# Unit-length removal keys of an RWKV-7 recurrence, moved from the recurrence units to the key and value stages

## The chip, the core and the metric

The kernel runs on one core of a Trainium2 chip. A core has five engines that run side by side, each working through its own instructions in order: TensorE (PE; PEld is its loading of weights), VectorE (DVE), ScalarE (ACT), GpSimd (POOL) and SyncE (SP), which here issues nearly all DMAs. They wait for each other through semaphores. The metric is the device time of one execution in microseconds; all times are from the profile, the runs or the trace.

## The reference

The model has two layers over 256 frames of 2048 channels (32 heads of 64), float32 throughout: an RWKV-7 time mixing layer and a forgetting-attention layer, each followed by a SwiGLU channel mixer. The change touches the time mixing, whose core is

```python
rkv = jnp.einsum('pbtc,pcd->pbtd', xm[:3], w_rkv)
r, k, v = rkv[0], rkv[1], rkv[2]
w_log = -jax.nn.softplus(-(w0 + jnp.tanh(xw @ w1) @ w2).astype(f32)) - 0.5
decay = jnp.exp(-jnp.exp(w_log))
a = jax.nn.sigmoid(a0 + (xa @ a1) @ a2)
g = jax.nn.sigmoid(xg @ g1) @ g2
kk = (k * k_k).reshape(B, T, H, N).astype(f32)
kk = kk / jnp.maximum(jnp.sqrt(jnp.sum(kk * kk, axis=-1, keepdims=True)), 1e-12)
k = k * (1.0 + (a - 1.0) * k_a)
...
y = wkv7_scan(rh, wh, kh, vh, -kk, kk * ah)
```

with the state update `S_t = S_{t-1} diag(w_t) + (S_{t-1} a_t) b_t^T + v_t k_t^T`, `y_t = S_t r_t`. The vector `kk` is the removal key: the direction in which the state forgets, scaled to unit length in each head.

## The kernel before

Every large product is a GEMM over weights that are streamed from DRAM. `Stream` (lines 58 to 185) holds a list of all GEMMs in order. SP loads pieces of 512 KB into three stage buffers `st`; each piece has two blocks of 128 x 512. ACT rounds a block to its high half `wh` (L149) and DVE makes the low half `wl` (L150), up to six blocks ahead of PE. For each block and each of two tiles of 128 frames PE does three matmuls (L182 to L184): high by high, high by low, low by high. After each such triple `tick` gives every active generator one step: this is how other work is woven into a GEMM. A `yield` ends a step. At most four generators are active in the key and value stages, eight later; others wait in a queue.

The program is then laid out by a scheduler, which takes the instructions with their dependencies and writes an order for each engine, so an instruction can stand some way from where its step was. The buffers of a pool are reused in turn; the wait for the last reader of a buffer is added by the framework.

The time mixing has these stages:

1. `begin` (L383) normalises the input, transposes it and makes the operands of the k GEMMs.
2. The GEMMs k0 to k3. `keep_k` copies their results to `K`. From k1 on `early` (L510) is woven in: the token-shift mix of the values (`xm`, L374 to L381), then three low-rank products (`lora`, L442), whose operands `xlh` and `xll` DVE and ACT make just ahead of the matmuls L464 to L466.
3. The GEMMs v0 to v3. The mix for r is woven in; the values go to DRAM (`vdram`, L545), and `centred` (L495) sends them once more, less their head means (`wdram`, L507).
4. The GEMMs r0 to r3 with the small decay and gate GEMMs, then the output projection. Into these four pipelines are woven over eight units, a unit being one column group `g` of 512 channels (eight heads) and one tile `t`: `prepare` (L580) makes the decays and the scaled operands of a unit, `solve` and `merge` invert its triangular systems, `chain` carries the state, `post` normalises the outputs. They pass on to each other through the set `done`.

In `prepare` a unit's removal keys take six operations: `kk` = k times `vk` (L594, DVE), its square (L596, ACT), the sum over a head (L610, DVE), a lower bound (L611, DVE), the power of -1/2 (L612, POOL) and the scaling (L633, DVE). L634 and L638 then use `kk`. `vk` is the group's row of the parameter `a_k_k`, broadcast over the partitions, loaded with `va` and `vr` when r is finished (L953). The buffer `kk` is there once, so a unit's `kk` can only be written when the unit before has read its own for the last time (L646).

The pools that matter: `pre` holds two buffers each of `f2` and `u2` (used by `begin`, `f2` also by `centred`), `lw` two of each small tile.

Of the kernel before, what the change touches and what calls it, by code (L numbers as in the profile page):

```python
# [8 lines left out]
F32 = mybir.dt.float32  # L9
F32R = mybir.dt.float32r  # L10
BF16 = mybir.dt.bfloat16
AF = mybir.ActivationFunctionType
ALU = mybir.AluOpType
AX = mybir.AxisListType
# [3 lines left out]
P = 128  # L18
T = 256
D = 2048  # L20
KT = D // P
H = 32
N = 64
# [184 lines left out]
def hybrid_kernel(ctx, tc, const, x, a_norm_g, a_mix, a_w_rkv, a_w0, a_w1, a_w2, a_a0, a_a1, a_a2,  # L208
# [127 lines left out]
    with ExitStack() as actx:  # L336
        a1 = actx.enter_context(tc.tile_pool(name="a1", bufs=1))
        rv = actx.enter_context(tc.tile_pool(name="rv", bufs=2))
        vdram = dram.tile([T, D], F32, name="vdram")
        wdram = dram.tile([T, D], F32, name="wdram")  # L340
        loraw = {}

        with ExitStack() as bctx:
# [151 lines left out]
            def centred(vt, at):  # L495
# [11 lines left out]
                nc.sync.dma_start(wdram[at], wt)  # L507

            def early():
                fetch()  # L510
                fetch()
                yield from differences()
                yield from mixed(2, xv, "xv")
                yield from lora(LORA, 3, lambda ps: halves("w", LORA, ps[0:LORA, 0:T], AF.Tanh))
                yield from lora(LORA, 4, lambda ps: halves("a", LORA, ps[0:LORA, 0:T]))
                yield from lora(GLORA, 5, gate_halves)
                done.add(("lora", 0))
# [19 lines left out]
            xr = pair("xa")  # L537
            S.add(mixed(0, xr, "xr"))
            for g in range(4):
                ps = S.gemm(f"v{g}", lhs_of(xv), ready=lambda kt: has("xv", kt))  # L540
                for t in range(2):
                    vt = rv.tile([P, 512], F32, name="rv")
                    nc.scalar.copy(vt[:, :], ps[t][:, :])
                    at = slice(t * P, (t + 1) * P), slice(g * 512, (g + 1) * 512)
                    nc.sync.dma_start(vdram[at], vt[:, :])  # L545
                    S.add(centred(vt, at))
            S.until(lambda: not S.act and not S.pend)

        with ExitStack() as bctx:
# [31 lines left out]
            def prepare():  # L581
                for i, (g, t) in enumerate(order):
                    yield from wait(("r", g))
                    tw, ta = wat[g][0][t], wat[g][1][t]
                    vk, va, vr = vec[g][:3]
                    k = K[g][:, t, :]
# [6 lines left out]
                    kk = u1.tile([P, 512], F32, name="kk")  # L593
                    nc.vector.tensor_tensor(kk[:, :], k, vk[:, :], op=ALU.mult)  # L594
                    sq = u1.tile([P, 512], F32, name="rr")
                    nc.scalar.activation(sq[:, :], kk[:, :], AF.Square)  # L596
                    yield
# [10 lines left out]
                    S.give(2)  # L608
                    n8 = u1.tile([P, 8], F32, name="n8")
                    nc.vector.tensor_reduce(n8[:, :], h4(sq[:, :]), AX.X, ALU.add)  # L610
                    nc.vector.tensor_scalar(n8[:, :], n8[:, :], 1e-24, None, op0=ALU.max)  # L611
                    nc.gpsimd.tensor_tensor(n8[:, :], n8[:, :], pw[:, :], op=ALU.pow)  # L612
                    yield
# [18 lines left out]
                    yield  # L632
                    nc.vector.tensor_tensor(h4(kk[:, :]), h4(kk[:, :]), n8[:, :].unsqueeze(2).broadcast_to([P, 8, N]), op=ALU.mult)  # L633
                    nc.vector.scalar_tensor_tensor(Wp, kk[:, :], -1.0, Wp, op0=ALU.mult, op1=ALU.mult)  # L634
# [236 lines left out]
            def post(i, g, t, Y, bon):  # L871
# [3 lines left out]
                yield from wait(("g2", g))  # L875
                vg, vb = vec[g][3:]
                b8 = lambda a: a.unsqueeze(2).broadcast_to([P, 8, N])
# [66 lines left out]
            for g in range(4):  # L944
# [4 lines left out]
                for t in range(2):  # L949
                    a = rv.tile([P, 512], F32, name="rv")  # L950
                    nc.scalar.copy(a[:, :], ps[t][:, :])
                    rts[g].append(a)
                vec[g] = [bc(v, g, nm) for v, nm in ((a_k_k[0], "vk"), (a_k_a[0], "va"), (a_r_k[0].rearrange("h n -> (h n)"), "vr"))]  # L953
                nc.scalar.mul(vec[g][1][:, :], vec[g][1][:, :], 0.5)
                ps = S.gemm(f"w2{g}", lambda kt: tuple(loraw["w"]))
# [451 lines left out]
```

## Time and profile before

| what | us |
|---|---|
| median of 3 runs | 2602.72 (2599.71 to 2609.24) |
| the profiled execution, its own time | 2608.68 |
| span of the profiled execution, first to last instruction | 2606.8 |
| PE busy | 2558.9 |
| DVE busy | 1693.5 |
| ACT busy | 1412.3 |
| POOL busy | 90.3 |
| the eight scalings L633 start at | 245.2 to 516.5 |

"Busy" is the time in which an engine had an instruction in work. Matmuls overlap, so PE can look busy while it is not at its pace; its pace is read from the number of matmuls in a stretch. A group's row gives its count, the shortest, median and longest duration in ns, and when the first and the last of it start. The chain of waits is followed back from the last instruction: at each step to what released it, or to the instruction before it on its engine. An engine's row of a wait names who ended it, its sum, how often, and the longest.

### The profile page before, as it was taken

The numbers are of one execution on the slowest core, as the hardware profiler recorded it, in microseconds if no ns is written. First come the engines' busy times: TensorE is split into PE (matmuls) and PEld (weight loads), VectorE is DVE, ScalarE is ACT, GpSimd is POOL, SyncE is SP. The second block draws the span as 40 slices with busy tenths as digits, with TensorE's granted clock in tenths as the row PEclk, the third lists the DMA queues.
The fourth block names the chain that finished last, engine by engine and source line by source line (L and its number), as shares of the span: only waits on it lengthen the run. The fifth ranks groups of instructions, "written<-read, shape, count | busy, mean of one in ns | idle before, by whom it ended". The sixth has DMA issues, their size and how long they took to land.

```text
span 2606.8 us, 40879 instructions
## 1 busy us (share of the span) xinstructions
PE 2558.9 (98%) x15160; PEld 2091.2 (80%) x15160; DVE 1693.5 (65%) x3041; ACT 1412.3 (54%) x2613; POOL 90.3 (3%) x73
## 2 busy tenths in 40 slices
PE   7999999999999999999999999999999999999998
PEld 5788777778888888888888788888888888888887
DVE  7886988977555555555556677676655555555554
ACT  6665665556454455545545565565654555454444
POOL 0000011100000000000001011010000000000000
PEclk9999999999999999999999999999999999999999
DMA  6667433446666666655566666664666666665554
GB/s 193 181 206 242 128 99 105 120 123 186 189 190 189 189 190 187 192 192 188 190 194 198 197 202 182 190 202 148 192 193 186 191 188 189 190 190 191 194 194 162
DMA packets 271095, 472.64 MB, mean 181 GB/s; under 512 B 39400, under 2 KB 49848, under 8 KB 270896
## 3 DMA queue, kind: packets, MB, share of 16 engines
q1 hardware_dynamic: 267600, 467.30, 59.1%
q10 hardware_dynamic: 3136, 2.74, 0.3%
q8 instruction: 119, 1.95, 0.3%
q14 instruction: 80, 0.66, 0.1%
q0 software_dynamic: 160, 0.00, 0.0%
HBM read 459.47 MB, written 6.32 MB: 179 GB/s over the span
## 4 chain that ended last, share of the span: by engine, by line
PE 86%; DVE 6%; DMA 3%; ACT 2%; issue 1%; POOL 1%; ACTq 0%; SPq 0%; POOLq 0%; DVEq 0%
PE mm L182 26%; PE mm L183 26%; PE mm L184 26%; DVE wl L150 2%; DMA st<-in_a_w_rkv_dram 1%; DMA st<-in_b_w_in_dram 1%; ACT wh L149 1%; PE bg L1010 1%; PE bg L854 1%; PE bg L312 1%; PE bg L836 0%; DVE xmf L377 0%; PE bg L1246 0%; PE bg L846 0%; DMA st<-in_a_w_o_dram 0%
## 5 line engine op out<-in xcount | busy, mean ns | idle before, releaser
L150 DVE TENSOR_TENSOR wl<-st,wh 128x512 fp32r<-128x512 f32 (+1 forms) x1648 | 1127.9, 689 | 802.3 <-ACT wh L149 797.0
L149 ACT CAST wh<-st 128x512 fp32r<-128x512 f32 (+1 forms) x1648 | 1017.0, 622 | 979.5 <-DVE wl L150 691.6
L182 PE MATMUL mm<-wh,xb 128*128 128x512 f32 x2048 | 803.5, 392 | 0.0
L184 PE MATMUL mm<-wh,xb 128*128 128x512 f32 x2048 | 799.8, 391 | 0.0
L183 PE MATMUL mm<-wl,xb 128*128 128x512 f32 x2048 | 799.4, 390 | 0.0
L182 PEld LDWEIGHTS mm<-wh,xb 128*128 128x128 f32 x2048 | 384.6, 188 | 79.6 <-issue 3.0
L184 PEld LDWEIGHTS mm<-wh,xb 128*128 128x128 f32 x2048 | 384.4, 188 | 79.4
L183 PEld LDWEIGHTS mm<-wl,xb 128*128 128x128 f32 x2048 | 384.7, 188 | 76.4
L182 PE MATMUL mm<-wh,xa 128*128 128x512 f32 x768 | 310.5, 405 | 0.0
L183 PE MATMUL mm<-wl,xa 128*128 128x512 f32 x768 | 305.1, 397 | 1.5 <-DVE wl L150 1.5
L184 PE MATMUL mm<-wh,xa 128*128 128x512 f32 x768 | 304.7, 397 | 0.0
L182 PE MATMUL mm<-wh,hb 128*128 128x512 f32 x448 | 174.3, 389 | 0.0
L183 PE MATMUL mm<-wl,hb 128*128 128x512 f32 x448 | 174.3, 389 | 0.0
L184 PE MATMUL mm<-wh,hb 128*128 128x512 f32 x448 | 174.3, 389 | 0.0
L184 PEld LDWEIGHTS mm<-wh,xa 128*128 128x128 f32 x768 | 145.6, 190 | 30.8 <-DVE xa L923 0.3
L182 PEld LDWEIGHTS mm<-wh,xa 128*128 128x128 f32 x768 | 145.7, 190 | 30.3 <-issue 1.0
L183 PEld LDWEIGHTS mm<-wl,xa 128*128 128x128 f32 x768 | 145.8, 190 | 29.8 <-DVE wl L150 3.2
L182 PEld LDWEIGHTS mm<-wh,hb 128*128 128x128 f32 x448 | 84.1, 188 | 17.6
L184 PEld LDWEIGHTS mm<-wh,hb 128*128 128x128 f32 x448 | 84.1, 188 | 17.5
L183 PEld LDWEIGHTS mm<-wl,hb 128*128 128x128 f32 x448 | 84.1, 188 | 17.3
L1194 POOL TENSOR_TENSOR n<-n,pw 128x8 f32<-128x8 f32 x24 | 46.3, 1932 | 411.9 <-DVE n L1193 411.9
L1237 ACT ACTIVATE sc<-sc,nm 128x128 f32<-128x128 f32 x64 | 28.7, 449 | 26.3 <-DVE nm L1236 26.3
(294 smaller groups left out, 1844.9 us busy)
## 6 DMA issues: line engine op xcount, KB each, us to landing
st<-in_f_w_gu_dram SPq DMA_DIRECT2D x352, 512.0 KB, 3.8
st<-in_f_w_d_dram SPq DMA_DIRECT2D x176, 512.0 KB, 3.7
st<-in_b_w_in_dram SPq DMA_DIRECT2D x128, 512.0 KB, 4.4
st<-in_a_w_rkv_dram SPq DMA_DIRECT2D x96, 512.0 KB, 4.4
st<-in_a_w_o_dram SPq DMA_DIRECT2D x32, 512.0 KB, 4.4
st<-in_b_w_o_dram SPq DMA_DIRECT2D x32, 512.0 KB, 4.2
cb<-cdram SPq DMA_DIRECT2D x4, 1024.0 KB, 8.9
x<-in_x_dram SPq DMA_DIRECT2D x12, 256.0 KB, 4.6
```

The source lines that it names most:

```text
L149: nc.scalar.copy(hi[:rows, :n], st)
L150: nc.vector.tensor_tensor(lo[:rows, :n], st, hi[:rows, :n].bitcast(F32), op=ALU.subtract)
L182: nc.tensor.matmul(ps[t][:, :n], xh[:rows, c], wh, start=b == 0, stop=False)
L183: nc.tensor.matmul(ps[t][:, :n], xh[:rows, c], wl, start=False, stop=False)
L184: nc.tensor.matmul(ps[t][:, :n], xl[:rows, c], wh, start=False, stop=b == kts - 1)
L312: nc.tensor.transpose(tp[:, i * T + t * P : i * T + (t + 1) * P], src[:, t, c : c + P], ident)
L854: mm(pb[half[1 - q], ps_], M[:, q * 8 + s_, 0:C], vu[:, hs], start=first, stop=first or p == 3)
L1010: nc.tensor.transpose(tp[:, j * P : (j + 1) * P], h[:, j * P : (j + 1) * P], ident)
L1194: nc.gpsimd.tensor_tensor(n8[:, :], n8[:, :], pw[:, :], op=ALU.pow)
L1237: nc.scalar.activation(sc[:, c], sc[:, c], AF.Exp, bias=nm[:, t : t + 1], accum_out=nm[:, 2 + t : 3 + t])
```

## The change

A unit's removal keys are no longer made in `prepare`. A new generator `removal(g)`, added four times after the k GEMMs (behind `early` and the mix for r), makes them for both tiles of a group and stores them in a DRAM tensor `kdram`. `prepare` loads a unit's part of it into `kk`. The operations are the same, but the broadcast row of `a_k_k` is loaded for each tile (eight times rather than four), into the buffer in which the product then stands, and `vk` goes.

```diff
+        kdram = dram.tile([T, D], F32, name="kdram")
...
+            def removal(g):
+
+                pair8 = lambda: pre.tile([P, 2, T], F32, name="u2")[:, :, :].rearrange("p i n -> p (i n)")
+                for t in range(2):
+                    kk = pair8()
+                    nc.sync.dma_start(kk, a_k_k[0][g * 512 : (g + 1) * 512].partition_broadcast(P))
+                    yield
+                    yield
+                    nc.vector.tensor_tensor(kk, K[g][:, t, :], kk, op=ALU.mult)
+                    sq = pre.tile([P, 2, T], F32, name="f2")[:, :, :].rearrange("p i n -> p (i n)")
+                    nc.scalar.activation(sq, kk, AF.Square)
+                    yield
+                    n8 = lw.tile([P, 8], F32, name="n8")
+                    k8 = kk.rearrange("p (h n) -> p h n", n=N)
+                    nc.vector.tensor_reduce(n8[:, :], sq.rearrange("p (h n) -> p h n", n=N), AX.X, ALU.add)
+                    nc.vector.tensor_scalar(n8[:, :], n8[:, :], 1e-24, None, op0=ALU.max)
+                    nc.gpsimd.tensor_tensor(n8[:, :], n8[:, :], pw[:, :], op=ALU.pow)
+                    for _ in range(6):
+                        yield
+                    nc.vector.tensor_tensor(k8, k8, n8[:, :].unsqueeze(2).broadcast_to([P, 8, N]), op=ALU.mult)
+                    nc.sync.dma_start(kdram[t * P : (t + 1) * P, g * 512 : (g + 1) * 512], kk)
+                    yield
...
             S.add(mixed(0, xr, "xr"))
+            for g in range(4):
+                S.add(removal(g))
...
                     kk = u1.tile([P, 512], F32, name="kk")
-                    nc.vector.tensor_tensor(kk[:, :], k, vk[:, :], op=ALU.mult)
-                    sq = u1.tile([P, 512], F32, name="rr")
-                    nc.scalar.activation(sq[:, :], kk[:, :], AF.Square)
+                    nc.sync.dma_start(kk[:, :], kdram[t * P : (t + 1) * P, g * 512 : (g + 1) * 512])
...
-                    n8 = u1.tile([P, 8], F32, name="n8")
-                    nc.vector.tensor_reduce(n8[:, :], h4(sq[:, :]), AX.X, ALU.add)
-                    nc.vector.tensor_scalar(n8[:, :], n8[:, :], 1e-24, None, op0=ALU.max)
-                    nc.gpsimd.tensor_tensor(n8[:, :], n8[:, :], pw[:, :], op=ALU.pow)
...
-                    nc.vector.tensor_tensor(h4(kk[:, :]), h4(kk[:, :]), n8[:, :].unsqueeze(2).broadcast_to([P, 8, N]), op=ALU.mult)
                     nc.vector.scalar_tensor_tensor(Wp, kk[:, :], -1.0, Wp, op0=ALU.mult, op1=ALU.mult)
...
-                vec[g] = [bc(v, g, nm) for v, nm in ((a_k_k[0], "vk"), (a_k_a[0], "va"), (a_r_k[0].rearrange("h n -> (h n)"), "vr"))]
-                nc.scalar.mul(vec[g][1][:, :], vec[g][1][:, :], 0.5)
+                vec[g] = [bc(v, g, nm) for v, nm in ((a_k_a[0], "va"), (a_r_k[0].rearrange("h n -> (h n)"), "vr"))]
+                nc.scalar.mul(vec[g][0][:, :], vec[g][0][:, :], 0.5)
```

The scheduler's order shows where the instructions stand now. First DVE at the change from k2 to k3 (low halves 47 to 51 of the weights). `xmf`, `xlh` and `xll` belong to the low-rank products; `wl<-xmf,wh` is the low half of one of their results. Before:

```order
L381 TENSOR_TENSOR xll<-xmf,xlh 128x256
L150 TENSOR_TENSOR wl<-st,wh 128x512 x3
L377 SCALAR_TENSOR_TENSOR xmf<-xx,gcol,hT 128x256
L150 TENSOR_TENSOR wl<-st,wh 128x512
L377 SCALAR_TENSOR_TENSOR xmf<-xx,gcol,hT 128x256
L479 TENSOR_TENSOR wl<-xmf,wh 96x256
L381 TENSOR_TENSOR xll<-xmf,xlh 128x256
L150 TENSOR_TENSOR wl<-st,wh 128x512
```

In the changed kernel (L518 is the product with a_k_k, L524 the sum, L525 the bound, L529 the scaling; `u` is the buffer of the keys, `n` the head norms, `x` is K):

```order
L518 TENSOR_TENSOR u_1500<-x_474,u_1500 128x512
L150 TENSOR_TENSOR wl<-st,wh 128x512
L518 TENSOR_TENSOR u_1502<-x_475,u_1502 128x512
L524 TENSOR_REDUCE n_1555<-f_1537 128x8
L150 TENSOR_TENSOR wl<-st,wh 128x512
L525 TENSOR_SCALAR n_1555<-n_1555 128x8
L524 TENSOR_REDUCE n_1559<-f_1540 128x8
L529 TENSOR_TENSOR u_1500<-u_1500,n_1555 128x512
L150 TENSOR_TENSOR wl<-st,wh 128x512
L525 TENSOR_SCALAR n_1559<-n_1559 128x8
L529 TENSOR_TENSOR u_1502<-u_1502,n_1559 128x512
L150 TENSOR_TENSOR wl<-st,wh 128x512
```

The first tiles of groups 0 and 1 go through together, with their eight operations among four low halves; POOL's power stands between L525 and L529 of the same tile.

Second, SP in v1, where the first values have been stored. Before:

```order
L545 DMA vdram<-rv 128x512
L194 DMA st<-in_a_w_rkv_dram 128x2x512
L545 DMA vdram<-rv 128x512
L194 DMA st<-in_a_w_rkv_dram 128x2x512
L507 DMA wdram<-f_1946 128x512
L507 DMA wdram<-f_1949 128x512
L194 DMA st<-in_a_w_rkv_dram 128x2x512 x2
L563 DMA vk<-in_a_k_k_dram 128x512
```

In the changed kernel:

```order
L530 DMA kdram<-u_1793 128x512
L194 DMA st<-in_a_w_rkv_dram 128x2x512
L515 DMA u_1933<-in_a_k_k_dram 128x512
L530 DMA kdram<-u_1852 128x512
L194 DMA st<-in_a_w_rkv_dram 128x2x512
L515 DMA u_1988<-in_a_k_k_dram 128x512
L589 DMA va<-in_a_k_a_dram 128x512
L530 DMA kdram<-u_1933 128x512
L589 DMA vr<-in_a_r_k_dram 128x512
L508 DMA wdram<-f_2024 128x512
L589 DMA vg<-in_a_lnx_g_dram 128x512
L194 DMA st<-in_a_w_rkv_dram 128x2x512
```

`u_1933` is the same buffer as `u_1793`, and `u_1988` the same as `u_1852`: each load has to follow the store ahead of it. The stores wait for the scaling on DVE, and the three weight loads stand among them.

Third, DVE in `prepare`, near the third unit. Before:

```order
L594 TENSOR_TENSOR kk<-x_474,vk 128x512
L150 TENSOR_TENSOR wl<-st,wh 128x512
L765 TENSOR_TENSOR Ti<-bg,Ti 128x256
L610 TENSOR_REDUCE n_3511<-rr 128x8
L767 STREAM_TRANSPOSE Tt<-Ti 128x256
L611 TENSOR_SCALAR n_3511<-n_3511 128x8
L150 TENSOR_TENSOR wl<-st,wh 128x512 x2
L618 SCALAR_TENSOR_TENSOR k_3574<-ta_3418,va 128x512
L625 TENSOR_TENSOR rr<-rv,vr 128x512
L619 SCALAR_TENSOR_TENSOR k_3574<-k_3574,x_474 128x512
L633 TENSOR_TENSOR kk<-kk,n_3511 128x512
```

In the changed kernel (`Ti` and `Tt` belong to the triangular systems, `k` is the unit's scaled key, `rr` and `bon` its bonus):

```order
L767 TENSOR_TENSOR El<-Dg,cst 128x256
L150 TENSOR_TENSOR wl<-st,wh 128x512 x3
L784 TENSOR_TENSOR Ti<-bg,Ti 128x256
L638 SCALAR_TENSOR_TENSOR k_3639<-ta_3489,va 128x512
L786 STREAM_TRANSPOSE Tt<-Ti 128x256
L150 TENSOR_TENSOR wl<-st,wh 128x512
L639 SCALAR_TENSOR_TENSOR k_3639<-k_3639,x_475 128x512
L645 TENSOR_TENSOR rr<-rv,vr 128x512
L646 TENSOR_TENSOR rr<-rr,k_3639 128x512
L648 TENSOR_REDUCE bon<-rr 128x8
```

The four operations on the removal keys are gone from the queue; those on `k` and `rr` follow one another directly.

More of the change, by code (lines that the diff above doesn't have):

```diff
@@ L584, in prepare @@
                     tw, ta = wat[g][0][t], wat[g][1][t]
-                    vk, va, vr = vec[g][:3]
+                    va, vr = vec[g][:2]
                     k = K[g][:, t, :]
@@ L875, in post @@
                 yield from wait(("g2", g))
-                vg, vb = vec[g][3:]
+                vg, vb = vec[g][2:]
                 b8 = lambda a: a.unsqueeze(2).broadcast_to([P, 8, N])
```

## The prediction

> **What bounds the kernel now.** I read the page first, for the shares and for the chain that ended last.
>
> ```profile
> span 2606.8 us, 40879 instructions
> PE 2558.9 (98%) x15160; PEld 2091.2 (80%) x15160; DVE 1693.5 (65%) x3041; ACT 1412.3 (54%) x2613; POOL 90.3 (3%) x73
> ...
> PE 86%; DVE 6%; DMA 3%; ACT 2%; issue 1%; POOL 1%; ACTq 0%; SPq 0%; POOLq 0%; DVEq 0%
> ```
>
> TensorE bounds the whole: 86% of the chain, VectorE 6%. The change gives PE nothing to do and takes nothing from it, so it can only move the time where PE waits for somebody. Next the table by stretch: the last k GEMM and the first v GEMMs (100 to 200 us), the recurrence units (257 to 577), and for comparison a stretch of the channel mixer.
>
> ```profile
> 100.00:120.00 20.00, 20.00 (x103) 16.64 (x102) 19.25 (x44) 14.48 (x32) 0.00 (x0) 1.00 0.59 176
> 120.00:140.00 20.00, 20.00 (x104) 16.53 (x103) 14.87 (x32) 13.00 (x29) 0.00 (x0) 1.00 0.60 186
> 140.00:160.00 20.00, 19.48 (x99) 15.85 (x100) 19.51 (x47) 13.48 (x30) 0.00 (x0) 1.00 0.43 130
> 160.00:180.00 20.00, 20.00 (x112) 16.76 (x111) 18.80 (x41) 12.14 (x27) 0.00 (x0) 1.00 0.79 240
> 180.00:200.00 20.00, 20.00 (x90) 16.57 (x89) 12.56 (x23) 9.80 (x18) 0.00 (x0) 1.00 0.88 291
> ...
> 257.00:577.00 320.00, 304.99 (x4764) 234.76 (x4763) 282.64 (x642) 195.27 (x417) 30.53 (x27) 0.97 0.41 118
> 700.00:740.00 40.00, 40.00 (x182) 33.04 (x181) 22.47 (x33) 20.10 (x33) 0.00 (x0) 1.00 0.66 192
> ```
>
> Behind the length of a stretch stand the busy times of PE, PEld, DVE, ACT and POOL, each with its count, then the granted clock and DMA's share and rate. In the mixer DVE has 22.47 of 40 us to do. In the units it has 282.64 of 320 (88%), which is the load that the change lightens. But from 100 to 180 us, where the change puts the work, it has 72.43 of 80 (91%): 7.57 us are free there, and 7.44 more from 180 to 200. The last row also gives PE's pace: 40 us / 182 = 0.22 us a matmul, so a weight block (two tiles, three matmuls each) lasts 1.32 us, and the six blocks that the low halves are made ahead cover 7.9 us.
>
> The chain of waits in that earlier stretch (100 to 190 us) shows whether DVE matters there:
>
> ```profile
> by line: PE mm L183 19.9%; PE mm L184 19.7%; PE mm L182 19.4%; DVE xmf L377 9.0%; DVE wl L150 6.9%; PE bg L464 5.7%; PE bg L465 4.7%; PE bg L466 4.6%; DVE xa L381 4.3%; DVE xll L381 2.3%; DVE ll L453 2.0%; issue 1.4%; ACT xlh L380 0.5%
> ```
>
> It does: 24.5% of the chain (9.0 + 6.9 + 4.3 + 2.3 + 2.0) are DVE, mostly the token-shift mixes. PE hardly stands still because DVE is just in time. And the waits of PE's weight loads from 100 to 180 us name the operand without a cushion:
>
> ```profile
> PEld bg L464 <- ACT xlh L380: 2.8, 7, 0.9
> PEld bg L466 <- DVE xll L381: 0.3, 2, 0.2
> ```
>
> The low-rank matmuls wait seven times for halves that DVE and ACT have only just made. The 7.9 us cushion is the weights' alone.
>
> **The change, part by part.** The six operations that leave a unit:
>
> ```profile
> L594 DVE TENSOR_TENSOR kk<-x,vk x8: 676/682/693, 238.9 to 491.8; 128x512 f32<-128x512 f32 x8
> L596 ACT ACTIVATE rr<-kk x8: 629/632/664, 239.6 to 492.5; 128x512 f32<-128x512 f32 x8
> L610 DVE TENSOR_REDUCE n<-rr x8: 643/675/686, 240.3 to 503.1; 128x8 f32<-128x512 f32 x8
> L611 DVE TENSOR_SCALAR n<-n x8: 128/160/164, 242.1 to 504.4; 128x8 f32<-128x8 f32 x8
> L612 POOL TENSOR_TENSOR n<-n,pw x8: 1636/1942/2011, 243.5 to 505.1; 128x8 f32<-128x8 f32 x8
> L633 DVE TENSOR_TENSOR kk<-kk,n x8: 676/680/693, 245.2 to 516.5; 128x512 f32<-128x512 f32 x8
> ```
>
> *Units: what is taken away.* What of it lies on the chain, the chain of waits shows in small windows:
>
> ```profile
> 306.10 0.31 DVE kk L633
> 333.35 0.60 DVE kk L594
> 336.43 0.59 DVE n L610
> 337.36 0.07 DVE n L611
> ...
> 369.54 0.60 DVE kk L594
> 373.97 0.59 DVE n L610
> 374.91 0.05 DVE n L611
> ...
> 407.43 0.59 DVE kk L594
> ```
>
> That is 3.4 us in all. The same rows show that one operation delays the next by less than its duration (0.60 against 0.68), so a unit's four DVE operations cost 0.60 + 0.59 + 0.07 + 0.60 = 1.86 us of the engine, the eight units 14.9. The gain lies between 0 (another wait is late next) and 14.9 (DVE sets the pace throughout). I take 3.4, the chain's own number; what is late next is the rest of DVE's queue. The Square (8 x 0.63 on ACT, 195 of 320 us busy) and pow are off the chain: nothing.
>
> Two rows say how long a transfer of 256 KB takes from its issue to its landing, the parameter loads (L563) and the store to wdram (L507):
>
> ```profile
> DMA to landing us min/median/max: 3.1/3.2/5.1
> DMA to landing us min/median/max: 2.6/4.9/5.1
> ```
>
> The unit's new load of kk stands thirteen steps ahead of its reader; a step is at least three matmuls (0.66 us), so 8.6 us cover these 3 to 5. On SP it waits until the old kk is read for the last time, and the state chain's loads of sv and vu and the next weights are behind it; the vk loads, of which four go, stood there in the same way. I take nothing; without that cover a unit would wait up to 5 us.
>
> *Key and value stages, first four tiles.* When a v GEMM ends, its rows are stored:
>
> ```profile
> L545 SPq DMA_DIRECT2D vdram<-rv x8: 339/405/492, 164.8 to 235.3; - x8
> ```
>
> So v0 ends at 164.8, and k3 and v0 are the 55 us or so before. The order puts the first four tiles at blocks 47 to 50 and 62 to 67 of DVE's low halves (16 blocks a GEMM), about 100 to 140 us. They cost 4 x 1.86 = 7.4 us of DVE, and waits for POOL: the first tile's pow (1.94) has one reduce (0.60) beside it, the second's scale stands right behind its max, 1.34 + 1.94; the next two have about 1.2 us beside them, 2 x 0.74. Together 12.2 us against 0.75 + 5.13 us of free time: 6.3 over. The weights' cushion of 7.9 us would hide all of it, the low-rank operands' lack of one would show all of it. Between 0 and 6.3 I take 3.5, since both kinds stand in that row of work.
>
> *Last four tiles (blocks 80 to 91: v1, 160 to 200 us).* 7.4 us of DVE against 1.20 + 7.44 free, but the last two tiles need their buffer back: its store has to land (4.9), then the row of a_k_k (3.2), 8.1 us, while DVE has some 6 us of other work between the two; 2 us of standing, and 1.6 for a pow with little beside it. 11.0 against 8.6: 2.4 over. On SP weight loads are queued behind these waits: between the first and the third weight load after the first store of this group stand two loads that wait for stores and two stores that wait for DVE; PE waits for those weights. Below nothing it can't go, since nothing leaves these stages. From 0 (the idle of 180 to 200 us hides it) to 15 (the rival below), I take 5: DVE's 2.4 and one weight piece late by its own two blocks' time (2.6).
>
> The Trainium skill (DMA: Bandwidth & Descriptors, Anatomy of one DMA) gives a transfer about 2.0 us and its bytes over 436 GB/s, fitted on the gpsimd path: an estimate of 2.6 us for these 256 KB, so store and load would take 5.2 us, DVE would not stand, and the sum would be 2 us lower. The landing rows above (4.9 and 3.2) disagree, and the measurement decides.
>
> POOL's pow itself might hold DVE up. A timeline of the units says no:
>
> ```profile
> 302.85 1.94 POOL L612 TENSOR_TENSOR n<-n,pw 128x8 f32<-128x8 f32 x1 [5.42 <-DVE n L611]
> ...
> 303.60 0.69 DVE L150 TENSOR_TENSOR wl<-st,wh 128x512 fp32r<-128x512 f32 x1 [0.31 <-ACT wh L149]
> ...
> 304.21 0.68 DVE L618 SCALAR_TENSOR_TENSOR k<-ta,va 128x512 f32<-128x512 f32 x1
> ```
>
> Two DVE operations with two SBUF inputs start inside one pow and take their usual 0.68. The Trainium skill (SBUF — State Buffer, SBUF: two separate sides) says that such an operation is blocked while a GpSimd operation that reads SBUF holds the shared port; by that the eight pows would add up to 8 x 1.94 = 15.5 us of DVE here, an estimate that this row contradicts.
>
> *Transfers.* Eight broadcast loads, eight stores and eight loads come, four loads go: 20 x 256 KB more. DMA's share is 0.43 to 0.88 in the table; nothing beyond the waits priced above.
>
> **The sum.** The profiled execution took 2608.68 us, its span 2606.8 and 1.9 around it. Plus 3.5, plus 5, minus 3.4 is plus 5.1: 2613.8. It lies 5.96 above the median of 2602.72; against that, 2607.8.
>
> **Rivals.** *Faster: DVE sets the pace of the units.* For it: 88% busy, and of the units' 320 us PE is busy 305 with a part of that stretched by waits. Against it: 3.4 us on the chain. If all 14.9 come back and the early stages hide half of their 8.5, the time is 2602.7 - 14.9 + 4.2 = 2592. It decides if PE's waits that DVE ends shrink by more than the chain's share.
>
> *Slower: SP's queue.* The load for the third use of a buffer stands until its store has landed (4.9), the store behind it until then, the next load for another 4.9, the next store until the loaded row has landed (3.2) and been worked on (0.68 + 0.63 + 0.68 + 0.16 + 1.94 + 0.68 = 4.8): about 17.8 us in which SP issues one or two weight pieces, where PE eats one in 2.6 us. Beyond the cushion of 7.9 this is 9.9, and the last store, waiting for the second tile's work, holds the next pieces some 5 us more: plus 15, with a gain of 3.4 in the units and the 3.5 from before 2618. For it: three stage buffers only; against it: the pieces behind could not have been issued earlier anyway while DVE holds the buffers. It decides where a weight piece lands more than 7.9 us after its turn.
>
> *The work only moves.* If neither stage has PE wait for these operations, the time stays at 2602.7.
>
> **Numbers.** The forecast gets 0.52, the faster rival 0.16, the slower 0.20, no movement 0.12. What a measurement of this kernel can tell from no change is about 0.5%, 13 us. Of the faster rival 0.10 goes past 2589.7 (early stages hide it all, gain of 13 and more); with a forecast centred near plus 5 and ends of minus 14.9 and plus 21.3 (6.3 and 15, no gain), slower by that much takes the slower rival, 0.20; the rest, 0.70, is the same. The range of 8 in 10 reaches into both rivals: 2590 to 2620.
>
> **What would show it.** Right: the units' DVE time falls by about 15 us, their stretch by 3 to 4; PE gets new waits between 100 and 200 us on low-rank operands and on weights, 5 to 12 us in all, and DVE shows waits for POOL at the scaling of the second tile. Wrong: PE at its old pace through v1 (the forecast is then too slow by 8.5), or a unit stretch shorter by 10 us or more, or waits of PE for weight pieces at v2 of more than 10 us.

## The result and the profile after

The changed kernel takes 2618.34 us in the median (2612.44 to 2624.2, six runs) against 2601.97 for the kernel before on the same chip: a ratio of 1.006, 95% interval [1.005, 1.007]. Run once more it took 2616.51 against 2602.73, ratio 1.005 [1.0035, 1.0066]. So the change costs 13 to 16 us. It has the forecast's sign but three times its size; it lies inside the stated range of 2590 to 2620, near its upper end, and it stands at the number that the prediction gave to the rival "SP's queue".

The profiled execution is the fastest of its six, 2612.44 us. Its span is only 3.9 us longer than that of the kernel before (2610.7 against 2606.8), whose profiled execution was one of its slowest; what such executions differ in is said under the hardware below. Its page has the shares first:

```profile
span 2610.7 us, 40925 instructions
PE 2554.6 (98%) x15160; PEld 2084.0 (80%) x15160; DVE 1695.3 (65%) x3041; ACT 1409.0 (54%) x2613; POOL 89.5 (3%) x73
...
PE 81%; DVE 5%; DMA 3%; ACT 3%; issue 1%; POOL 0%; POOLq 0%; ACTq 0%; DVEq 0%; SPq 0%
```

The work of each engine is what it was (DVE 1693.5 before, 1695.3 now, both in 3041 instructions). Only its place has changed, so the loss has to be waiting. The table by stretch, with the same columns and edges as before, shows where:

```profile
100.00:120.00 20.00, 17.98 (x84) 14.65 (x85) 18.76 (x43) 12.30 (x27) 0.00 (x0) 0.91 0.67 204
120.00:140.00 20.00, 20.00 (x105) 16.65 (x104) 18.59 (x40) 13.75 (x31) 3.24 (x2) 1.00 0.75 232
140.00:160.00 20.00, 19.83 (x101) 15.93 (x100) 19.85 (x49) 13.94 (x32) 0.00 (x0) 1.00 0.41 134
160.00:180.00 20.00, 18.08 (x99) 14.76 (x98) 17.68 (x37) 11.23 (x24) 3.89 (x2) 1.00 0.70 209
180.00:200.00 20.00, 16.97 (x67) 12.49 (x67) 12.89 (x28) 7.12 (x15) 6.18 (x5) 0.91 0.71 235
...
257.00:577.00 320.00, 302.49 (x4739) 231.84 (x4738) 274.12 (x616) 193.46 (x413) 18.31 (x20) 0.99 0.43 126
```

Two rows have changed most: 100 to 120 (84 matmuls where there were 103) and 180 to 200 (67 where there were 90). In both, the granted clock is 0.91 where it was 1.00. In the row between, 160 to 180, PE lost 1.9 us of busy time and 13 matmuls. In the units' row DVE has 274.12 us to do instead of 282.64; over the 256 matmuls of the column "units" below it falls from 317.3 to 306.6. The units are no faster, as the second pair of traces shows (367.1 and 367.3).

PE's waits for its weight loads from 100 to 180 us, and, for the power on POOL (L526), its row and who waited for it:

```profile
PEld bg L465 <- ACT xlh L381: 7.3, 9, 2.7
PEld bg L467 <- DVE xll L382: 1.1, 3, 0.7
```

```profile
L526 POOL TENSOR_TENSOR n<-n,pw x8: 1637/1694/3622, 94.8 to 187.1; 128x8 f32<-128x8 f32 x8
...
  DVE u L529: 6.8, 6
```

The low-rank operands made PE wait 2.8 us before and 7.3 now; DVE's scaling (L529) stood 6.8 us in all, in six of eight tiles, for POOL.

To have one measure for all runs I take, from the one trace of each, the time from the first matmul of L182 in one GEMM to the first in the next; "units" is the time from r0's first over the next 256 matmuls of L182. Each ratio is to runs of the kernel before on the same chip. us:

| kernel | k1 | k2 | v0 | v1 | v2 | v3 | units | ratio to before, 95% |
|---|---|---|---|---|---|---|---|---|
| before (shown run) | 29.5 | 27.6 | 30.3 | 26.8 | 21.8 | 21.8 | 366.5 | |
| again_before | 27.6 | 27.6 | 30.4 | 26.9 | 21.8 | 21.8 | 367.1 | 0.9995 [0.9985, 1.0005] |
| changed | 26.4 | 31.8 | 30.0 | 34.3 | 22.3 | 21.8 | 363.1 | 1.006 [1.005, 1.007] |
| again_after | 26.7 | 31.9 | 30.2 | 34.2 | 22.4 | 21.8 | 367.3 | 1.005 [1.0035, 1.0066] |
| add_alone | 27.1 | 31.9 | 30.6 | 34.1 | 21.8 | 21.8 | 366.9 | 1.0054 [1.0042, 1.0067] |
| take_alone | 29.1 | 27.6 | 30.4 | 26.7 | 21.8 | 21.8 | 364.6 | 0.9999 [0.9988, 1.001] |
| dve_only | 27.7 | 29.0 | 32.7 | 28.7 | 21.8 | 21.8 | 368.9 | 1.0029 [1.0015, 1.0043] |
| dma_only | 29.0 | 27.6 | 30.0 | 27.9 | 21.8 | 21.8 | 363.8 | 1.0012 [1.0003, 1.0021] |
| pool_queue | 28.3 | 32.3 | 32.0 | 36.5 | 22.4 | 21.8 | 366.4 | 1.0078 [1.0065, 1.009] |
| late | 26.5 | 27.6 | 30.2 | 27.0 | 21.8 | 30.4 | 375.1 | 1.007 [1.0056, 1.0084] |
| no_pow | 29.0 | 27.8 | 30.1 | 31.8 | 22.4 | 21.8 | 375.1 | 1.0038 [1.0025, 1.0051] |
| free_load | 28.6 | 32.1 | 30.2 | 32.2 | 22.4 | 21.8 | 366.0 | 1.005 [1.0033, 1.0066] |
| sing_v1 | 26.3 | 27.7 | 30.7 | 27.5 | 23.6 | 27.2 | 370.6 | 1.0067 [1.0051, 1.0083] |
| twice | 28.2 | 27.6 | 30.3 | 26.8 | 21.8 | 21.8 | 376.1 | 1.0044 [1.0028, 1.0059] |

k0 (26.9 to 28.4) and k3 (26.7 or 26.8) are left out. The columns k1 and units differ by some us between executions of one kernel, with the spells of half clock that fell into them (more on that below); the other columns repeat within 0.6 us wherever two kernels have the same work there. One execution of take_alone, 2847.95 us at a granted clock of 0.845, is left out of its ratio. Most of the change's cost is in two GEMMs: k2 plus 4.2, v1 plus 7.4.

### The profile page after: what moved, and what is told of

Its sections match the earlier page's. It is cut to its first block, busy times and chain, and to the rows that moved or that the text cites. A ratio compares the mean times of both kernels' runs of the same rounds, so it can differ in the third digit from the quotient of the medians.

```text
span 2610.7 us, 40925 instructions
## 1 busy us (share of the span) xinstructions
PE 2554.6 (98%) x15160; PEld 2084.0 (80%) x15160; DVE 1695.3 (65%) x3041; ACT 1409.0 (54%) x2613; POOL 89.5 (3%) x73
## 3 DMA queue, kind: packets, MB, share of 16 engines
q8 instruction: 119, 1.95, 0.3%
## 4 chain that ended last, share of the span: by engine, by line
PE 81%; DVE 5%; DMA 3%; ACT 3%; issue 1%; POOL 0%; POOLq 0%; ACTq 0%; DVEq 0%; SPq 0%
PE mm L182 25%; PE mm L184 25%; PE mm L183 25%; DVE wl L150 2%; DMA st<-in_a_w_rkv_dram 2%; ACT wh L149 1%; PE bg L1029 1%; PE bg L873 1%; DMA va<-in_a_k_a_dram 1%; PE bg L312 1%; PE bg L1265 0%; PE bg L855 0%; PE bg L865 0%; PE bg L871 0%; DVE xb L676 0%
## 5 line engine op out<-in xcount | busy, mean ns | idle before, releaser
L182 PE MATMUL mm<-wh,xb 128*128 128x512 f32 x2048 | 803.8, 393 | 0.0
L182 PEld LDWEIGHTS mm<-wh,xb 128*128 128x128 f32 x2048 | 385.1, 188 | 80.0 <-issue 3.3
L182 PE MATMUL mm<-wh,xa 128*128 128x512 f32 x768 | 311.4, 406 | 0.8 <-ACT tw L978 0.8
L182 PE MATMUL mm<-wh,hb 128*128 128x512 f32 x448 | 174.3, 389 | 0.0
L182 PEld LDWEIGHTS mm<-wh,xa 128*128 128x128 f32 x768 | 144.9, 189 | 31.3 <-issue 1.3
L182 PEld LDWEIGHTS mm<-wh,hb 128*128 128x128 f32 x448 | 84.1, 188 | 17.5
L1256 ACT ACTIVATE sc<-sc,nm 128x128 f32<-128x128 f32 x64 | 28.7, 449 | 26.6 <-DVE nm L1255 26.6
```

The source lines that it names most:

```text
L182: nc.tensor.matmul(ps[t][:, :n], xh[:rows, c], wh, start=b == 0, stop=False)
L1256: nc.scalar.activation(sc[:, c], sc[:, c], AF.Exp, bias=nm[:, t : t + 1], accum_out=nm[:, 2 + t : 3 + t])
```

## The experiments

**The two halves of the change.** Theory A is the prediction's: the cost arises in the key and value stages and the units give a little back. Its rival B: the units themselves got slower, by the new loads. Three kernels and the kernel before once more tell them apart.

again_after: the changed kernel, nothing edited.

> The changed kernel once more, for more times and a second trace. Its first trace shows v1 lasting 34.3 us against 26.7 before, k3 and v0 as before, the units from r0 on 3.4 us shorter, and a span only 3.9 us longer, while the medians of the first runs are 16.4 us apart. Theory A (the cost lies in the key and value stages and changes from execution to execution): v1 or the GEMMs around it are longer here by 10 to 20 us than in the trace of before, the units again 3 us shorter. Theory B (the cost lies in the units, where the order of all engines has moved, and the first trace caught a good execution): v1 is again 7 to 8 us longer, and the units are 5 to 12 us longer than in the trace of before. Time in both: 2614 to 2622.

add_alone: the kernel before with the generator, whose stored keys nobody reads; the units still make their own.

```diff
+        kdram = dram.tile([T, D], F32, name="kdram")
+            def removal(g):
...
+            for g in range(4):
+                S.add(removal(g))
```

> The kernel before with the new generator added and its result stored and never read: the units make their own keys as before. Theory A: the whole cost is in it and the units' gain of 3.4 is missing, so plus 17 to plus 22 us against before (2619 to 2624). Theory B: plus 7 to 9 (2609 to 2611), the longer v1 and nothing else.

take_alone: the changed kernel without the generator. The units load `kk` from a weight matrix in DRAM instead, so their removal keys are not the right ones; every load, wait and instruction of a unit is as in the changed kernel.

```diff
-            for g in range(4):
-                S.add(removal(g))
...
-                    nc.sync.dma_start(kk[:, :], kdram[t * P : (t + 1) * P, g * 512 : (g + 1) * 512])
+                    nc.sync.dma_start(kk[:, :], a_w_o[0][t * P : (t + 1) * P, g * 512 : (g + 1) * 512])
```

> The changed kernel without the new generator: the units load 128 x 512 values of the output weights in the place of the removal keys, so the recurrence is computed with other keys and the unit's six operations are left out. The key and value stages are those of before. Theory A: minus 3 to minus 6 us (2596 to 2599). Theory B: plus 5 to plus 12 (2607 to 2614). If VectorE set the pace of the units (the rival of the prediction) it would be minus 12 to minus 15 (2587 to 2590).

again_before: the kernel before against itself.

> The kernel before once more, for a second trace: whether the stretches of its first trace (k1 29.5, k2 27.6, k3 26.8, v0 30.3, v1 26.7 us, and 366.5 from r0 to the end of the output projection) come back. Both theories expect each within 3 us and the units within 6; the time is 2600 to 2609.

Measured: add_alone 2616.0 us against 2602.73 (1.0054), take_alone 2602.29 (0.9999), again_before 2601.37. The generator alone costs 13.3 us in the medians, what the change costs within the noise; taking the work out of the units brings nothing that can be seen: minus 0.3 us by the ratio, interval minus 3.1 to plus 2.6. Both times lie between the ranges of the two theories. Theory A is right on the place of the cost and wrong on the gain. In the table by GEMM, add_alone is the changed kernel's twin (31.9 and 34.1).

Where the units' gain went, the waits from 240 to 577 us show. First DVE's and ACT's for the streamed weights in the kernel before:

```profile
DVE wl L150 <- ACT wh L149: 12.9, 15, 2.5
```

```profile
ACT wh L149 <- PE mm L184: 28.9, 33, 2.2
```

and the same two of take_alone:

```profile
DVE wl L150 <- ACT wh L149: 24.9, 22, 2.4
```

```profile
ACT wh L149 <- PE mm L184: 44.9, 39, 2.7
```

DVE has 14.9 us less to do and waits 12.0 us longer for a high half; ACT waits 16.0 us longer for PE to be done with a buffer of weights. The time that DVE won, it spends waiting ahead of PE; PE does not get on faster by it.

**What in the generator costs.** Theory D: DVE's own time (8 x 1.86 us and the waits for POOL). Theory S: SP, where weight pieces stand behind the generator's loads and stores. dve_only is add_alone without its DMAs (the product is K times K, so nothing is loaded; nothing is stored); dma_only is add_alone with the loads and stores alone, the row of a_k_k itself being stored.

```diff
-                    nc.sync.dma_start(kk, a_k_k[0][g * 512 : (g + 1) * 512].partition_broadcast(P))
-                    nc.vector.tensor_tensor(kk, K[g][:, t, :], kk, op=ALU.mult)
+                    nc.vector.tensor_tensor(kk, K[g][:, t, :], K[g][:, t, :], op=ALU.mult)
...
-                    nc.sync.dma_start(kdram[t * P : (t + 1) * P, g * 512 : (g + 1) * 512], kk)
```

> Added alone once more (plus 13 there: k2 31.9, v1 34.1 us, against 27.6 and 26.8 before), without its transfers: the product is K times K, and the scaled keys go nowhere, so loads and stores of the generator are left out; the units are those of before. Theory D (VectorE's time: 14.9 us of operations and the waits for POOL's power don't fit into the 7.6 us free from 100 to 180 us): plus 10 to plus 14, k2 at 31 to 32 and v1 at 32 to 34. Theory S (SyncE's queue: weight loads stand behind loads that wait for stores and stores that wait for the scaling): plus 4 to plus 6, k2 as in added alone, v1 back to 28.

> Added alone with the transfers only: the broadcast row is loaded and stored again after the same number of steps, and the four VectorE operations, the square and the power are left out (what is stored is not the key; the units are those of before). Theory D: 0 to plus 2. Theory S: plus 6 to plus 10, most of it in v1.

pool_queue is the changed kernel, with the generator's DMAs issued by GpSimd.

```diff
-                    nc.sync.dma_start(kk, a_k_k[0][g * 512 : (g + 1) * 512].partition_broadcast(P))
+                    nc.gpsimd.dma_start(kk, a_k_k[0][g * 512 : (g + 1) * 512].partition_broadcast(P))
...
-                    nc.sync.dma_start(kdram[t * P : (t + 1) * P, g * 512 : (g + 1) * 512], kk)
+                    nc.gpsimd.dma_start(kdram[t * P : (t + 1) * P, g * 512 : (g + 1) * 512], kk)
```

> The changed kernel with the generator's eight loads and eight stores issued by GpSimd instead of SyncE, so that no weight load stands behind them. Theory D: as the change, plus 12 to plus 16, v1 33 to 35. Theory S: plus 4 to plus 7, v1 27 to 29; k2 still 31 to 32 in both.

late is the changed kernel, with the four generators as two chains that are added before v2, where DVE has 7.4 of 20 us free.

```diff
+            def removals(g):
+                yield from removal(g)
+                yield from removal(g + 1)
...
-            for g in range(4):
-                S.add(removal(g))
             for g in range(4):
+                if g == 2:
+                    S.add(removals(0))
+                    S.add(removals(2))
                 ps = S.gemm(f"v{g}", lhs_of(xv), ready=lambda kt: has("xv", kt))
```

> The changed kernel with the generator moved behind v1: two chains of two groups each, woven into v2 and v3, where VectorE has 22 of 60 us free (the table of before, 180 to 220, and the same again). Theory D: all of it fits, minus 2 to plus 3, with k2 at 28 to 29 and v1 at 27. Theory S: the turn-round of the two buffers costs there what it cost in v1, plus 6 to plus 10, in v2 and v3.

Measured: dve_only 2610.43 us (1.0029), dma_only 2605.16 (1.0012), pool_queue 2622.68 (1.0078), late 2623.11 (1.007). DVE's part is the larger, and in the medians the two halves (8.4 and 3.1 us) add up to 11.5 of add_alone's 13.3. But k2's 4.2 us and v1's 7.4 are in neither half: dve_only has 1.4 and 1.9 there (and 2.4 in v0), dma_only 0 and 1.1. In dve_only the order on DVE differs from add_alone's from 41 us on, so it is not a clean half; the loss of k2 and v1 comes with both halves, or with this order, and these two runs do not say which. And pool_queue and late, each made to help by one theory, took longer than the changed kernel (plus 20.7 and 21.1 us). Both theories missed all four times.

late's chain of waits shows the shape (start, us, what), from 201 to 226 us, in v3:

```profile
201.81 0.70 DVE u L529
202.53 2.50 DMA kdram<-u
...
205.05 6.17 DMA u<-in_a_k_k_dram
...
211.95 0.68 DVE wl L150
212.63 1.19 DVE n L524 x2
213.82 0.09 DVE n L525
...
215.96 1.64 POOL n L526
...
220.03 5.53 DMA u<-in_a_k_k_dram
```

Scaling, store, load of the next row into the same buffer, product, sum, bound, power: one tile's turn follows on the other's in a buffer, and weights are in between. No engine is full here (DVE is busy 28.02 of 48 us from 192 to 240); it is the turn that takes long. pool_queue has the same turn with POOL's own queue in it, where loads and stores stand in line with the powers, so it does not test SP's queue by itself: there DVE stood 4.4 us for the loaded row from 90 to 240 us, against 0.5 in add_alone.

**Two parts of the turn, taken away one at a time.** no_pow is add_alone without the power, so that what is stored has not unit length; free_load is the changed kernel with the row loaded into the buffer of the squares, which comes free at the sum, rather than into that of the keys, which comes free when its store has landed.

```diff
-                    nc.gpsimd.tensor_tensor(n8[:, :], n8[:, :], pw[:, :], op=ALU.pow)
```

> The kernel before plus the generator (its result stored and not used, as in add_alone), without the power on GpSimd: the keys are scaled by the bounded sum itself, so what is stored is not of unit length. Theory P: DVE's wait for POOL is what hurts the first tiles. It stood 2.9 us there, the next low-rank half came 2.5 us late, PE stood 2.3 us and ran at half clock for the 3.4 us after. Without the power the GEMM k2 is back at 27.6 us (from 31.9), v1 at 31 to 33 (from 34.1), and the +13.3 of add_alone becomes +7 to +9: 2609 to 2611. Theory D: DVE's own time, 8 x 1.86 us, is what counts, and it is still there: k2 at 30 or more, +12 to +13, about 2614 to 2615.

```diff
-                    kk = pair8()
-                    nc.sync.dma_start(kk, a_k_k[0][g * 512 : (g + 1) * 512].partition_broadcast(P))
+                    sq = pre.tile([P, 2, T], F32, name="f2")[:, :, :].rearrange("p i n -> p (i n)")
+                    nc.sync.dma_start(sq, a_k_k[0][g * 512 : (g + 1) * 512].partition_broadcast(P))
                     yield
                     yield
-                    nc.vector.tensor_tensor(kk, K[g][:, t, :], kk, op=ALU.mult)
-                    sq = pre.tile([P, 2, T], F32, name="f2")[:, :, :].rearrange("p i n -> p (i n)")
+                    kk = pair8()
+                    nc.vector.tensor_tensor(kk, K[g][:, t, :], sq, op=ALU.mult)
                     nc.scalar.activation(sq, kk, AF.Square)
```

> The changed kernel, with the row of a_k_k loaded into the buffer of the squares instead of that of the keys: a load then waits for the sum of the tile two before it and no longer for that tile's power, scaling and store. Nothing is left out. Theory T: the last tiles pay for a buffer's turn (store, load, product, sum, power, scaling, store), during which weight pieces stand behind loads and stores on SP. v1 falls from 34.2 us to 28 to 30, k2 stays at 32, and the time is 2610 to 2612. Theory P or D: the turn is not what costs; v1 stays at 33 to 34 and the time at 2615 to 2617.

Measured: no_pow 2611.26 us against 2602.45 (1.0038, ten runs). k2 is back at 27.8, v1 at 31.8. In its row for 100 to 120 us PE is at its pace and the clock at 1.00, with more DVE work in it than the kernel before has (19.98 against 19.25):

```profile
100.00:120.00 20.00, 20.00 (x102) 16.44 (x101) 19.98 (x46) 14.09 (x32) 0.00 (x0) 1.00 0.77 235
```

Up to the end of k2 at 108 us DVE, ACT and PE work in the same order in add_alone and in no_pow, so only the power differs. So k2's loss is the wait for POOL, and DVE's own time is free there: theory P, in k2. In v1 the power is 2.3 of the 7.4 us. free_load: 2615.8 us (1.005); k2 unchanged, v1 32.2. Theory T was right that the load's wait for the store is part of v1's loss, but it is 2 us of it, too little to see in the total, and its times were missed. The units' 375.1 us in no_pow's profiled execution contain two spells of half clock, 13.7 and 17.1 us long; its median is the better witness.

**The place.** sing_v1 is free_load with the four generators as one, added before v1. The order then has one tile in k2 and the other seven singly, at low halves 94 to 129: the end of v1, v2 and v3.

```diff
+            def removals():
+                for g in range(4):
+                    yield from removal(g)
...
-            for g in range(4):
-                S.add(removal(g))
             for g in range(4):
+                if g == 1:
+                    S.add(removals())
```

> The changed kernel with the row loaded into the buffer of the squares, as in free_load, and the four generators run one after the other as one, added before v1 rather than before v0. The order then has one tile at low half 47 and the other seven singly at 94 to 129, mostly in v2 and v3 where DVE has seven of twenty us to spare. Nothing is left out. Theory W (the cost is tiles in lockstep where DVE has no room: POOL's power and a buffer's turn then become waits of PE, each with a spell of half clock behind it): k2 28 to 30 us, v1 27 to 29, v2 and v3 together at most +3, and 2603 to 2607 in all. Theory Q (wherever the generator stands, its waits on SP hold weight pieces up, as late showed in v3 and behind it): v2, v3 and the units' start pay instead, +13 to +21, 2615 to 2623.

Measured: 2620.12 us against 2602.08 (1.0067). As theory W said, k2 is at 27.7 and v1 at 27.5; but v2, v3 and the units take 1.8, 5.4 and about 4 more, and theory Q's total is the right one. What is short there stands in ACT's waits from 192 to 240 us. Before:

```profile
ACT wh L149 <- DVE wl L150: 9.0, 13, 0.8
ACT wh L149 <- PE mm L184: 8.3, 9, 2.1
ACT wh L149 <- DMA st<-in_a_w_rkv_dram: 5.1, 4, 2.1
```

sing_v1:

```profile
ACT wh L149 <- DMA st<-in_a_w_rkv_dram: 19.3, 8, 5.2
```

and in the table by stretch, before and sing_v1:

```profile
192.00:240.00 48.00, 48.00 (x213) 39.75 (x212) 31.61 (x55) 24.08 (x41) 2.00 (x3) 1.00 0.77 252
```

```profile
192.00:240.00 48.00, 42.96 (x181) 33.06 (x180) 31.75 (x60) 21.92 (x40) 8.80 (x5) 1.00 0.83 274
```

DVE has room in v2 and v3, but the weights have none: PE uses them at its full pace, and ACT waits 19.3 us for pieces where it waited 5.1. DVE's room was room of the wrong engine. Whether the pieces come late because they stand behind the generator's loads and stores on SP, as theory Q has it, or because the DMA engines have more to move (0.83 busy for 0.77) is not separated.

**The units from the other side.** twice is the kernel before with a unit's four DVE operations done twice (the product, the sum and the bound once more into the same place, the scaling once more into a dead buffer), 14.9 us more of DVE.

```diff
+                    nc.vector.tensor_tensor(kk[:, :], k, vk[:, :], op=ALU.mult)
                     nc.vector.tensor_tensor(kk[:, :], k, vk[:, :], op=ALU.mult)
...
+                    nc.vector.tensor_reduce(n8[:, :], h4(sq[:, :]), AX.X, ALU.add)
+                    nc.vector.tensor_scalar(n8[:, :], n8[:, :], 1e-24, None, op0=ALU.max)
...
+                    nc.vector.tensor_tensor(h4(rr[:, :]), h4(kk[:, :]), n8[:, :].unsqueeze(2).broadcast_to([P, 8, N]), op=ALU.mult)
```

> The kernel before, with a unit's four VectorE operations on the removal keys done twice (product, sum and bound once more into the same place, the scaling once more into a dead buffer): 8 x 1.86 = 14.9 us more of DVE in the units, as much as the change takes away. Nothing is left out. Theory N (DVE has room in the units, as the about zero of take_alone says): at most +2, 2601 to 2604. Theory C (what stood on the chain counts, 3.4 us): +3 to +5, 2605 to 2607. Theory G (DVE sets the pace of the units, and take_alone's gain was lost to something else): +10 to +15, 2612 to 2617.

Measured: 2612.81 us against 2602.45 (1.0044 [1.0028, 1.0059]): 7 to 15 us of the 14.9 come out as time. Theories N and C are refuted and G's number is right, though G's second half (that take_alone's gain was lost to something else) is not shown by it. Some 4 of the 9 us that the column "units" grows are spells of half clock, 27.3 us of them where the two traces of the kernel before have 17.1 and 20.5. Together the two runs say that the units sit on an edge: more DVE work costs time, less brings none. That PE and its weights are what comes next is read from take_alone's rows and was not tested. What the new loads of `kk` cost in take_alone was not measured by itself, so a small gain that they eat is not excluded; within its interval take_alone leaves 3.1 us for it at the most.

## Why the prediction was right, and where it was not

**What bounds the kernel: right.** DVE was the engine without room from 100 to 180 us, and the low-rank operands the ones without a cushion. The new waits are on just these (7.3 us at L465).

**First four tiles, plus 3.5 taken, 0 to 6.3 allowed: the wait was right, the sum was not; 4.2 measured.** The prediction named the scaling right behind its max, 1.34 + 1.94. DVE's timeline in k2 has it:

```profile
96.52 0.69 DVE L529 TENSOR_TENSOR u<-u,n 128x512 f32<-128x512 f32 x1 [1.18 <-POOL n L526]
...
97.73 0.17 DVE L525 TENSOR_SCALAR n<-n 128x8 f32<-128x8 f32 x1
99.65 0.69 DVE L529 TENSOR_TENSOR u<-u,n 128x512 f32<-128x512 f32 x1 [1.75 <-POOL n L526]
100.25 0.68 DVE L150 TENSOR_TENSOR wl<-st,wh 128x512 fp32r<-128x512 f32 x1
100.86 0.48 DVE L378 SCALAR_TENSOR_TENSOR xmf<-xx,gcol,hT 128x256 f32<-128x256 f32 x1
```

1.18 + 1.75 = 2.93 us of standing; the mix L378 is late by it. PE in five small windows around it (length, PE busy and count, granted clock, DMA share, rate):

```profile
96.00:99.50 3.50, 3.50 (x17) 1.00 0.27 92
99.50:101.80 2.30, 0.05 (x1) 1.00 0.88 259
...
102.50:105.90 3.40, 3.20 (x11) 0.50 0.63 159
105.90:109.30 3.40, 3.40 (x19) 0.99 0.84 256
```

PE stands 2.3 us, and a little later its clock is at one half for 3.4 us, in which it does 11 matmuls for 19 in the window behind. The spell is 1.7 us of work: 2.3 + 1.7 = 4.0 of k2's 4.2. The sum had no term for it. The other half of this step, the tiles in v0, cost nothing (30.0 against 30.3). DVE's own 7.4 us, the largest term of the sum, did not count: no_pow has k2's tiles without the power at no cost, and v0's cost nothing as they are. That 3.5 came near 4.2 is therefore in part luck.

**Last four tiles, plus 5 taken, 0 to 15 allowed: mis-sized, 7.4 in v1 and 0.5 in v2 measured.** PE stood 1.9 us from 160 to 180, and from 183 us on (PE, PEld, DVE, ACT, POOL, clock, DMA's share and rate):

```profile
183.00:188.00 5.00, 2.79 (x14) 1.86 (x14) 4.60 (x11) 2.26 (x6) 1.32 (x2) 0.99 0.67 227
188.00:191.30 3.30, 3.30 (x9) 2.23 (x7) 1.77 (x4) 0.45 (x2) 3.30 (x4) 0.50 0.73 209
```

2.2 us of standing, again a half-clock spell, worth 1.7, and 0.6 us of standing behind it at 191.5: 6.4 of the 7.4 in all. The buffer's turn was there as priced. add_alone's chain, from the scaling of the fifth tile to the product of the seventh, which takes its buffer:

```profile
169.83 0.61 DVE u L529
...
170.46 5.00 DMA kdram<-u
...
175.47 4.38 DMA u<-in_a_k_k_dram
...
179.94 0.69 DVE u L518
```

That is 9.4 us for store and load where the prediction put 8.1. But DVE stood only 0.3 us for the row in the changed kernel, not 2; it was ACT that stood, for weight pieces. Its row from 100 to 200 us, before and after:

```profile
ACT wh L149 <- DMA st<-in_a_w_rkv_dram: 12.0, 8, 2.8
```

```profile
ACT wh L149 <- DMA st<-in_a_w_rkv_dram: 18.2, 8, 4.3
```

The Trainium skill (DMA: Bandwidth & Descriptors, Anatomy of one DMA) would have the two transfers in an estimated 5.2 us; the chain, with 9.4, disagrees.

**Units, minus 3.4 taken, 0 to 14.9 allowed: the step that failed.** It held that what of the removed work lies on the chain comes back, "what is late next is the rest of DVE's queue". Nothing came back that can be seen (take_alone, minus 3.1 to plus 2.6); what is late next is, by take_alone's rows, PE and the weights ahead of it. The chain showed where those 3.4 us were, not what would end last without them. That the range's lower end was zero was right. The shown executions do have the units 3.4 us apart (366.5 and 363.1), just the gain that was forecast, but that is chance: their spells of half clock last 17.1 us before and 6.8 after, worth 8.5 and 3.4 us.

**The sum.** Predicted 3.5 + 5 - 3.4 = 5.1. By GEMM: 4.2 + 7.9 + 0 = 12.1, and 14 to 16 in the medians. Of the difference the missing gain is 3.4, the two spells of half clock another 3.4, for which the prediction had no term, though the granted 0.97 in the units' row of the kernel before was a sign of such spells. The units do not stay quite at 0: the column less half the time of its spells is 357.9 and 356.9 us for the two traces before, 356.1 for take_alone, 359.6 and 360.4 for the changed kernel and 360.1 for add_alone. So the generator seems to cost the units 2 to 3 us as well, for a reason that no run shows; with them the sum comes to the medians.

**The rivals.** The faster one is out (take_alone). The slower one had the right time, 2618, for a reason that holds only in part: the load's wait for the store is 2 us of v1 (free_load), all transfers alone are 3 us (dma_only). Taking them off SP made it worse, but put them in line with the powers on POOL, so SP's part in v1 is not measured by itself. "The work only moves" is out as well.

What stays open: v1's rest. no_pow leaves 5.0 us of it and free_load 5.4; the two together were not tried.

## What to carry to other kernels

A stage in which an engine idles is not free room: in v2 and v3 DVE had 7 of 20 us to spare, but the stream of weights had none, and in k2 a wait of 2.9 us for another engine cost 4 us where DVE's own work on the same tiles cost nothing. Before moving work, ask for each stage which supply is just in time, and count the moved chain's latency there (buffer, transfer, other engines), not only its busy time. And what a chain of waits shows of an operation (3.4 us here) need not come back when the operation goes (nothing seen here): test it by taking the operation away alone.

## What the runs showed of the hardware

PE's granted clock falls to one half for a while, mostly after PE has stood: behind the 2.3 us from 99.5 to 101.8, behind the two short stands from 183 to 188, and between 296 and 317 us in 13 of 14 traces, behind a gap of two to three us at the units' start; take_alone has a gap of 2.5 us there and no spell. But for those at a program's start and end, the spells last 3.4, 6.8, 10.2, 13.7 or 17.1 us in the traces, whole multiples of 3.41, and in each trace their starts lie whole multiples of 3.413 us apart (in the changed kernel's at 102.53, 187.87, 307.33 and 464.35 us: 25, 35 and 46 times). The Trainium skill (TensorE: Matmul & The Clock Gate, Part 1: The HAM clock gate) names a free-running window of 3413 ns, which these lengths bear out; but it lets the clock fall after an idle window of about 3.4 us, and here 2.3 us without a matmul were enough.

Which gap gets a spell, and how long a one, differs between executions (near 70 us 6.8 us of it in the shown run of before, 3.4 in again_before, none in the changed kernel, at gaps of 3.7, 2.5 and 2.7 us). The traces show what goes with it: how much PE stands within one of the windows of 3.413 us that these starts mark. In the window ahead of the changed kernel's spells at 102.53 and 307.33 us PE was busy 1.14 and 0.64 of 3.41 us; take_alone's gap of 2.5 us falls on two windows, with 2.23 and 2.08 us busy. Of all such windows at full clock from 60 to 600 us in the 14 traces, each one with PE busy under 1.48 us (33 of them) has a spell behind it, of those with 1.48 to 2.1 us 18 of 41, and of the busier ones 12 of 2052, for a reason not shown. So where a gap falls in the windows, which no kernel here controls, is part of its price.

Each such spell is worth 1.7 us or more of PE's work, and spells go with much of the spread of single runs (2612.44 to 2624.2 for the changed kernel). From the granted clock of each run, its time multiplied by one minus the clock is the time lost; over 63 runs of the kernel before it goes with the run's time with a correlation of 0.77, over the changed kernel's eleven with 0.92. In the mean it is 10.7 us before and 13.3 after, 2.6 more, close to the 3.4 of the two new spells.

POOL's power on 128x8 took 1.64 to 1.95 us in seven of eight tiles and 3.62 in the one at 187.05 us, 2.8 us of which lie in the half-clock spell from 187.87 on. It comes again in again_after (3.62 us) and, at 2.95 us, in add_alone. The spell alone does not make it: in twice a power lies 1.45 us in a spell and takes 2.01 us. What does is not shown.
